# Chunk 7 of the first FFN in seven block products instead of eight, with its gate row spread later

## The chip, the cores and the metric

One core of one Trainium2 chip runs the whole program. The metric is the device time of one execution in microseconds (us). The engines are TensorE (PE in the profile, PEld its weight loads), VectorE (DVE), ScalarE (ACT), GpSimd (POOL) and SyncE (SP), whose queue issues nearly all loads of weights.

## The reference, cut to what matters

A decoder trunk of two layers over 256 tokens of width 2048, in float32. Layer 0 mixes by pooling, layer 1 by attention; each layer ends in a SwiGLU FFN of 5632 channels, and every part has a shift, a scale and a gate that are computed from a conditioning vector `c`:

```python
def swiglu(h, w_gate, w_up, w_down):
    return (jax.nn.silu(h @ w_gate) * (h @ w_up)) @ w_down
...
shift_m, scale_m, gate_m, shift_f, scale_f, gate_f = jnp.split(sc @ mod_w[i] + mod_b[i], N_MOD, axis=-1)
...
h = modulate(rmsnorm(x, norm_ffn[i]), shift_f, scale_f)
x = x + gate_f[:, None, :] * swiglu(h, ffn_gate[i], ffn_up[i], ffn_down[i])
```

The change lies in the FFN of layer 0 (`i == 0`). `gate_f` is the gate of the title; its row of 2048 numbers is the same for all tokens.

## The kernel before

**Tiles.** The 256 tokens are two token tiles of 128. The width of 2048 is four blocks `j` of 512, and the 5632 channels are 11 chunks `c` of 512. A weight block of 512x512 is one unit: 1 MB is loaded on SP's queue into one of six `raw` buffers, ACT copies its upper part (`hi`, L381) and DVE subtracts to get the lower part (`lo`, L383), each into one of six `hl` buffers. PE then makes three products (upper by upper, upper weight by lower activation, lower weight by upper activation) of four 128-deep slices for two token tiles: 24 matmuls of 128x128 by 128x512 (`proj_unit`, L406). In the last unit of a bank the first token tile's 12 matmuls come first, so that the lower part is wanted sooner.

**Order of the FFN.** A written list sets it: `p1 p0 t1 p2 t0 p3 t2 p4 p5 d0 t3 t4 p6 t5 d1 p7 t6 p8 t7 p9 t8 d2 p10 t9 d3`. `p` projects a chunk by the gate and the up weights (8 units from chunk 6 on; of chunks 0 to 5 all but the last `j` was done earlier), and DVE multiplies the silu of the one by the other (L1005). `t` turns a chunk's result so that its channels lie on the partitions: chunks 6 to 8 of layer 0 go through memory by DMAs on POOL's queue (L560, L783) and are then split (L775, L776), the others are turned by PE (L794) and split from its bank by ACT (L797) and DVE (L798). `d` multiplies a group of chunks ([0,1,2], [3,4,5], [6,7,8], [9,10]) by the down weights, and DVE adds the bank to the running sum in `x` (L807; ACT copies it in the first group, L805). Instructions are ordered by a scheduler at build time that goes by the order of the code; the splits (L381, L383) and `minus` (L879) are raised by a fixed priority. Work put on the list `pending` is written behind a later split: with the number n, n splits later.

**Background work.** The rows for later parts are computed meanwhile: `Part.unit` loads 1 MB on SP's queue into a `raw` buffer, and DVE multiplies and sums it in one instruction of 128x2048 (L222). There are 84 such units in this FFN. `tick()` at each split issues as many as a rate says, which `plan` sets as the units there are over FFN0_UNITS (87) splits.

**Seven products.** In layer 1, chunks 6 to 10 go another way (`project_in_seven`): over the two token tiles, the blocks `j` 0 and 1, and the two weights gate and up, a 2x2 by 2x2 product of blocks is made in seven block products of 12 matmuls (`seventh`, L870) instead of eight; blocks 2 and 3 stay four plain units (`whole`). So 84 + 96 = 180 matmuls stand in place of 192. It needs four differences of raw weight blocks on DVE (`minus`, 128x2048), eleven splits instead of eight, four ACT copies of single products (`kept`: L889, L899, L902, L906), and sums of token tiles. These splits don't tick. `token_sums` makes the sums of tiles once a layer, in the first down group: 14 DVE operations of 128x512 and 4 ACT copies, pended 2, 4, 6 and 8 splits on. They take an `act` buffer and the one `gate` buffer.

**The gate's row.** `gate_to` makes the row and spreads it over 128 partitions by a DMA of 1 MB on POOL's queue (L303), in layer 0 as soon as the row is there. Layer 0's sum in `x` is multiplied by it in eight DVE operations of 128x512 in `known` (L647), which are pended at the last chunk. In layer 1 (`LATE_GATES`) the load is put off until behind the seven-product chunks, and the products with the gate come behind the additions of the third down group (L979).

Of the kernel before, what the change touches and what calls it, by code (L numbers as in the profile page):

```python
# [14 lines left out]
ALU = mybir.AluOpType  # L15
AX = mybir.AxisListType

P = 128
T = 256
NT = T // P  # L20
D = 2048
# [5 lines left out]
DEPTH = 2  # L27
# [32 lines left out]
GROUPS = ([0, 1, 2], [3, 4, 5], [6, 7, 8], [9, 10])  # L60
BLOCK = 32
TURNED_BY_DMA = (range(6, 9), range(10))
SEVEN = (range(0), range(6, 11))

WIDE = 64
AM, GM = 1, 2
# [1 line left out]
GM_BY_PE = (3, 0, 1)  # L68
PAIRS = 2

LATE_GATES = ("ffn1",)

BEGUN = 6
ASIDE = 5

FFN0_UNITS, MLA_UNITS, DQ_UNITS, WO_UNITS, FFN1_UNITS = 87, 4, 6, 8, 60
DOWN_UNITS = 23

KNOWN = (1, 3, 5, 7, 9, 10, 11, 12)
# [28 lines left out]
def tile_trunk(ctx: ExitStack, tc: tile.TileContext, a: dict, out: bass.AP):  # L108
# [162 lines left out]
    pending = []  # L271
# [13 lines left out]
    def gate_to(name, first):  # L285

        col = cols[:, C_SM0, :]
        row = dram.tile([KD, P], F32, name=nm("row"))

        def spread():  # L290
            pt = ps_t()
            pe.transpose(pt[:KD, :P], col, ident)
            turned = t2k([KD, P])
            act.activation(turned, pt[:KD, :P], AF.Copy)
            act.dma_start(row, turned)
            if name in LATE_GATES:
                late_gates.append(load)
            else:
                load()

        def load():
            gates[name] = s_row if name in LATE_GATES else gate_t([P, D])
            pool.dma_start(gates[name], row.rearrange("k q -> (k q)")[None, :].to_broadcast([P, D]))  # L303

        def done(sums):
            dve.tensor_tensor(out=col, in0=sums, in1=bias(first, KD), op=ALU.add)
            pending.append((1, spread))
        return done
# [319 lines left out]
    class StreamEnd:  # L628
# [6 lines left out]
        def start(self, gate):  # L635
# [3 lines left out]
            if l == DEPTH - 1:  # L639
                self.fn = act_t([P, D], F32)  # L640
                sync.dma_start(self.fn, a["final_norm"][None, :].to_broadcast([P, D]))
        def known(self, j, tok, gate):

            js = slice(j * CH, (j + 1) * CH)
            part, piece = self.parts[tok][:, js], x[:, tok, js]
            if self.l == 0:
                dve.tensor_tensor(out=piece, in0=piece, in1=gate[:, js], op=ALU.mult)  # L647
            dve.tensor_tensor(out=part, in0=piece, in1=part, op=ALU.add)

        def piece(self, bank, tok, j):  # L650
# [107 lines left out]
    def ffn(l, hT, gate_name, begun, then):  # L758
# [169 lines left out]
        def down(i):  # L928
            g = GROUPS[i]
            last = g[-1] == NF - 1  # L930
            if i == 0 and len(SEVEN[l]):
                release(0, DOWN_UNITS)
                token_sums()
            if last:
                stat_start()
# [2 lines left out]
            for j in range(ND):  # L938
# [34 lines left out]
                for tok in range(NT):  # L973
                    if last:
                        pending.append((0, lambda bank=banks[tok], tok=tok, j=j: end.piece(bank, tok, j)))
                    else:
                        pending.append((0, lambda bank=banks[tok], sums=x[:, tok, js]: gather(bank, sums, i == 0)))
                        if gate_name in LATE_GATES and i == len(GROUPS) - 2:
                            pending.append((1, lambda sums=x[:, tok, js], gate=gates[gate_name][:, js]: dve.tensor_tensor(  # L979
                                out=sums, in0=sums, in1=gate, op=ALU.mult)))  # L980

        def project_chunk(c):
            if c == ASIDE:
                stream_aside(l)
            if c == NF - 1:
                end = StreamEnd(l)
                stream_end.append(end)
                for n, wait in enumerate(KNOWN):
                    pending.append((wait, lambda n=n: end.known(n // NT, n % NT, gates[gate_name])))
            if c in SEVEN[l]:  # L990
                nat[c] = project_in_seven(c)
                if c == GROUPS[-1][0]:
                    late_gates.pop()()
                if c in TURNED_BY_DMA[l]:
                    pending.append((0, lambda: turn_blocks(c)))
                return
# [1076 lines left out]
```

## Time and profile before

| what | value |
|---|---|
| time, median of 3 runs | 1870.15 us (1869.64 to 1870.22) |
| the profiled execution's own time | 1870.4 us |
| its span in the profile | 1868.6 us |
| granted TensorE clock, mean | 0.992 |
| TensorE busy | 1818.7 us, 97% |
| VectorE busy | 1537.7 us, 82% |
| ScalarE busy | 878.0 us, 47% |

The span is one execution between its first and its last instruction on the chip; the 1.8 us beside it lie around the program. A row of a timeline gives the start, the duration, engine, line, operation, what is written from what, shapes and count, and in brackets how long the engine had been idle and who released it. Times in a timeline are from the span's start. DVE instructions overlap a little, so what one costs a queue is the distance from its start to the next one's.

### The profile page before, as it was taken

The page shows a single profiled execution, that of the slowest core. Times are in us where ns is not written, and L with a number is a line of the kernel's source. Part 1 is how long each engine was busy: PE and PEld are TensorE (multiplying, and loading weights), DVE is VectorE, ACT ScalarE, POOL GpSimd, SP SyncE. Part 2 cuts the span into 40 slices and gives each one's busy share as a digit, 9 for nine tenths or more (in the row PEclk, how much of TensorE's full clock was granted, in tenths as well). Part 3 has the DMA queues.
Part 4 walks back from the last instruction along what each step waited for, and adds up shares of the span by engine and source line. Part 5 has one row for each costly group of instructions (what it writes and reads, how often), then busy time and mean ns, then how long its engine had stood idle before and what let it go on. Part 6 is the DMA issues. An engine that isn't in the chain of part 4 may idle for free.

```text
span 1868.6 us, 21673 instructions
## 1 busy us (share of the span) xinstructions
PE 1818.7 (97%) x8506; PEld 1480.1 (79%) x8506; DVE 1537.7 (82%) x1528; ACT 878.0 (47%) x955; POOL 67.8 (4%) x98
## 2 busy tenths in 40 slices
PE   6769999999999999999999999999999999999998
PEld 2537888888888888888889888888888888887886
DVE  1458898899889798997798885888789887898696
ACT  3225543443433343344766735643445553655353
POOL 0000000000000000000100000100011000000000
PEclk9989999999999999999999999999999999999999
DMA  9999999889999899996495394998788687458651
GB/s 391 422 422 420 415 371 339 317 310 369 409 351 421 349 400 390 393 422 231 167 382 195 132 365 172 404 380 342 299 313 321 244 325 281 180 208 319 238 225 46
DMA packets 85192, 592.27 MB, mean 317 GB/s; under 512 B 10033, under 2 KB 10465, under 8 KB 16225
## 3 DMA queue, kind: packets, MB, share of 16 engines
q1 hardware_dynamic: 79202, 570.68, 77.8%
q0 software_dynamic: 5648, 19.93, 2.9%
q8 instruction: 66, 1.08, 0.2%
q10 hardware_dynamic: 240, 0.29, 0.0%
q14 instruction: 36, 0.29, 0.0%
HBM read 576.15 MB, written 14.70 MB: 316 GB/s over the span
## 4 chain that ended last, share of the span: by engine, by line
PE 91%; DMA 4%; DVE 3%; ACT 0%; issue 0%; SPq 0%; POOL 0%; POOLq 0%; DVEq 0%; ACTq 0%
PE ps L406 73%; PE ps L870 4%; PE ps L416 2%; DMA raw<-in_mod_shift_dram 1%; PE ps L1672 1%; PE ps L249 1%; PE ps L1354 1%; DMA raw<-in_mod_scale_dram 1%; DVE hl L383 1%; DMA raw<-in_mod_wt_dram 1%; PE ps L1758 1%; PE ps L1864 1%; DVE raw L222 1%; DMA raw<-in_mod_gate_dram 1%; PE ps L1575 1%; PE ps L1214 1%
## 5 line engine op out<-in xcount | busy, mean ns | idle before, releaser
L406 PE MATMUL ps<-hl,act 128*128 128x512 f32 x6096 | 1391.3, 389 | 0.3 <-DVE act L776 0.2
L406 PEld LDWEIGHTS ps<-hl,act 128*128 128x128 f32 x6096 | 1142.6, 188 | 238.7 <-DVE act L776 0.6
L381 ACT ACTIVATE hl<-raw 128x2048 fp32r<-128x2048 f32 x297 | 566.8, 1917 | 549.0 <-PE ps L406 260.1
L383 DVE TENSOR_TENSOR hl<-raw,hl 128x2048 fp32r<-128x2048 f32 x297 | 676.2, 2285 | 119.0 <-ACT hl L381 118.5
L222 DVE SCALAR_TENSOR_TENSOR raw<-raw,s_row 128x2048 f32<-128x2048 f32 x184 | 419.1, 2282 | 3.0 <-DMA raw<-in_mod_wt_dram 2.9
L249 PE MATMUL ps<-raw,s_strip 128*32 128x512 f32 x320 | 49.0, 709 | 26.1 <-DMA raw<-in_mod_shift_dram 17.2
L870 PE MATMUL ps<-hl,act 128*128 128x512 f32 x300 | 71.6, 390 | 0.0
L741 DVE TENSOR_TENSOR act<-ps,act 128x512 f32<-128x512 f32 x80 | 53.4, 681 | 15.2 <-PE ps L406 15.1
L870 PEld LDWEIGHTS ps<-hl,act 128*128 128x128 f32 x300 | 56.2, 188 | 11.9 <-DVE hl L383 0.2
L416 PE MATMUL ps<-hl,act 128*128 128x512 f32 x192 | 47.7, 401 | 0.6 <-DVE act L512 0.5
L249 PEld LDWEIGHTS ps<-raw,s_strip 128*32 128x32 f32 x320 | 7.8, 119 | 50.6 <-issue 21.4
L879 DVE TENSOR_TENSOR raw<-raw,raw 128x2048 f32<-128x2048 f32 x20 | 45.7, 2284 | 0.3
L1214 PE MATMUL ps<-act,act 128*128 128x256 f32 x128 | 33.6, 421 | 11.5 <-issue 11.5
L1214 PEld LDWEIGHTS ps<-act,act 128*128 128x128 f32 x128 | 26.2, 211 | 21.9 <-issue 17.1
L416 PEld LDWEIGHTS ps<-hl,act 128*128 128x128 f32 x192 | 35.1, 188 | 10.3 <-ACT act L499 2.5
L560 POOL DMA_DIRECT2D turned<-t2k x32 | 17.8, 556 | 613.5 <-DVE t2k L558 613.2
L739 ACT ACTIVATE act<-ps 128x512 f32<-128x512 f32 x32 | 19.1, 597 | 38.2 <-PE ps L406 38.2
L436 ACT ACTIVATE junk<-x 128x512 bf16<-128x512 f32 x23 | 14.5, 629 | 45.7 <-DVE x L655 28.6
L529 DVE TENSOR_TENSOR hl<-raw,hl 128x2048 fp32r<-128x2048 f32 (+3 forms) x17 | 31.9, 1878 | 4.8 <-ACT hl L526 4.7
L807 DVE TENSOR_TENSOR x<-ps,x 128x512 f32<-128x512 f32 x32 | 21.5, 686 | 12.5 <-PE ps L406 12.5
L870 PE MATMUL ps<-hl,gate 128*128 128x512 f32 x120 | 29.4, 393 | 0.6 <-ACT hl L381 0.6
L1179 DVE COPY hl<-ps 128x256 f32<-128x256 f32 x4 | 1.7, 424 | 32.3 <-PE ps L1178 32.3
(277 smaller groups left out, 1217.7 us busy)
## 6 DMA issues: line engine op xcount, KB each, us to landing
raw<-in_mod_wt_dram SPq DMA_DIRECT2D x152, 1024.0 KB, 7.6
raw<-in_ffn_down_dram SPq DMA_DIRECT2D x88, 1024.0 KB, 6.8
raw<-in_ffn_gate_dram SPq DMA_DIRECT2D x86, 1024.0 KB, 6.7
raw<-in_ffn_up_dram SPq DMA_DIRECT2D x86, 1024.0 KB, 6.9
raw<-in_kv_mod_wt_dram SPq DMA_DIRECT2D x32, 1024.0 KB, 8.5
raw<-in_mod_shift_dram SPq DMA_DIRECT2D x16, 1024.0 KB, 12.4
raw<-in_w_o_dram SPq DMA_DIRECT2D x16, 1024.0 KB, 6.4
raw<-in_mod_gate_dram SPq DMA_DIRECT2D x12, 1024.0 KB, 12.5
```

Source lines behind the costliest of these rows:

```text
L222: dve.scalar_tensor_tensor(out=r, in0=r, scalar=1.0, in1=s_row, op0=ALU.mult, op1=ALU.mult, accum_out=self.sums[:, self.n:self.n + 1])
L249: pe.matmul(self.bank[m * STRIP:(m + 1) * STRIP, :], lhsT=s_strip[:, self.kt + k, :], rhs=r[:, k, i, :], start=first, stop=last)
L381: hi_ins = act.activation(hi, r, AF.Copy)
L383: lo_ins = dve.tensor_tensor(out=lo, in0=r, in1=hi.bitcast(F32), op=ALU.subtract)
L406: pe.matmul(banks[tok], lhsT=t_[:, i, k, tok * P:(tok + 1) * P], rhs=w[:, k, :], start=first and n < len(part), stop=last and n >= len(ord ...
L416: pe.matmul(bank, lhsT=t_[:, i, k, tok * P:(tok + 1) * P], rhs=w[:, k, :], start=first and n == 0, stop=last and n == len(order) - 1)
L529: dve.tensor_tensor(out=w[2][:, ks], in0=w[0][:, ks], in1=w[1][:, ks].bitcast(F32), op=ALU.subtract)
L741: dve.tensor_tensor(out=part, in0=self.banks[tok], in1=part, op=ALU.add)
L807: dve.tensor_tensor(out=sums, in0=bank, in1=sums, op=ALU.add)
L870: pe.matmul(bank, lhsT=a_(i, k), rhs=w[:, k, :], start=first and n == 0, stop=last and n == len(order) - 1, skip_group_check=read)
L879: dve.tensor_tensor(out=out, in0=a_, in1=b_, op=ALU.subtract)
L1214: pe.matmul(mixed[g][:, n % 2, :], lhsT=wp[g][:, k, ns], rhs=pool_all[g // 2][:, g % 2, k, :], start=k == 0, stop=k == KL - 1)
```

## The change

Layer 0's chunk 7 goes by `project_in_seven` too, `token_sums` runs in layer 0's first down group, and the splits that tick are 8 fewer, for which FFN0_UNITS goes from 87 to 79. The token sums take the `gate` buffer in layer 0 as well; so the spreading of the gate's row is put off until `p7`, and the eight products with the gate move from `known` into the third down group, as they stand in layer 1. In layer 0 the background list isn't empty, so `kept` are four buffers of their own.

```diff
-SEVEN = (range(0), range(6, 11))
+SEVEN = (range(7, 8), range(6, 11))
...
-LATE_GATES = ("ffn1",)
+LATE_GATES = ("ffn0", "ffn1")
...
-FFN0_UNITS, MLA_UNITS, DQ_UNITS, WO_UNITS, FFN1_UNITS = 87, 4, 6, 8, 60
+FFN0_UNITS, MLA_UNITS, DQ_UNITS, WO_UNITS, FFN1_UNITS = 79, 4, 6, 8, 60
...
-            gates[name] = s_row if name in LATE_GATES else gate_t([P, D])
+            gates[name] = s_row if name == "ffn1" else gate_t([P, D])
...
-        def known(self, j, tok, gate):
+        def known(self, j, tok):
...
-            if self.l == 0:
-                dve.tensor_tensor(out=piece, in0=piece, in1=gate[:, js], op=ALU.mult)
             dve.tensor_tensor(out=part, in0=piece, in1=part, op=ALU.add)
...
-            if i == 0 and len(SEVEN[l]):
-                release(0, DOWN_UNITS)
+            if i == 0:
+                if l == DEPTH - 1:
+                    release(0, DOWN_UNITS)
                 token_sums()
...
-                        if gate_name in LATE_GATES and i == len(GROUPS) - 2:
+                        if i == len(GROUPS) - 2:
                             pending.append((1, lambda sums=x[:, tok, js], gate=gates[gate_name][:, js]: dve.tensor_tensor(
...
-                if c == GROUPS[-1][0]:
+                if c == min(SEVEN[l][-1], GROUPS[-1][0]):
                     late_gates.pop()()
```

Below, the order of instructions is shown at three places; names carry running numbers, and from L648 on, line numbers of the changed kernel are two lower than before, and from L933 on one lower.

**DVE from the end of the first down group into chunk 6, before.** The `hl` tiles are the lower parts of the last down unit (3199) and the first four units of chunk 6 (3264, 3299, 3332, 3365), `act` tiles on L798 the turned chunks 3 and 4.

```order
L383 TENSOR_TENSOR hl_3199<-raw_3193,hl_3198 128x2048
L222 SCALAR_TENSOR_TENSOR raw_3195,sums_2981<-raw_3195,s_row 128x2048
L798 TENSOR_TENSOR act_3241<-ps_3242,act_3241 128x4x128
L798 TENSOR_TENSOR act_3241<-ps_3249,act_3241 128x4x128
L383 TENSOR_TENSOR hl_3264<-raw_3258,hl_3263 128x2048
L222 SCALAR_TENSOR_TENSOR raw_3260,sums_2981<-raw_3260,s_row 128x2048
L383 TENSOR_TENSOR hl_3299<-raw_3293,hl_3298 128x2048
L222 SCALAR_TENSOR_TENSOR raw_3295,sums_2981<-raw_3295,s_row 128x2048
L383 TENSOR_TENSOR hl_3332<-raw_3326,hl_3331 128x2048
L222 SCALAR_TENSOR_TENSOR raw_3328,sums_2981<-raw_3328,s_row 128x2048
L383 TENSOR_TENSOR hl_3365<-raw_3359,hl_3364 128x2048
```

The same stretch now, from behind the last down unit's lower part (`hl_3228`) to that of chunk 6's second unit (`hl_3328`; the third and fourth are `hl_3361` and `hl_3394`); L820 writes the lower half of a sum of tiles, L825 to L840 make the sums.

```order
L383 TENSOR_TENSOR hl_3228<-raw_3222,hl_3227 128x2048
L820 TENSOR_TENSOR act_2810<-t2k_2971,act_2810 128x512
L825 TENSOR_TENSOR t2k_3122<-act_943 128x512
L839 TENSOR_TENSOR t2k_2971<-act_1371,t2k_2971 128x512
L826 TENSOR_TENSOR t2k_3121<-t2k_3121,t2k_3122 128x512
L840 TENSOR_TENSOR t2k_2971<-t2k_2971,act_1371 128x512
L383 TENSOR_TENSOR hl_3293<-raw_3287,hl_3292 128x2048
L820 TENSOR_TENSOR gate_2811<-t2k_2971,gate_2811 128x512
L820 TENSOR_TENSOR gate_2811<-t2k_3121,gate_2811 128x512
L222 SCALAR_TENSOR_TENSOR raw_3224,sums_2928<-raw_3224,s_row 128x2048
L796 TENSOR_TENSOR act_3255<-ps_3256,act_3255 128x4x128
L383 TENSOR_TENSOR hl_3328<-raw_3322,hl_3327 128x2048
```

Seven operations of the token sums stand between these splits, and the halves of the turned chunks 3 and 4 (L796) come behind chunk 6's first units. Between `hl_3328` and `hl_3394` follow three L796, one L222, the split of `hl_3361`, and two L222 in a row.

**ACT at the start of chunk 7, before:** the upper parts of its first units, and nothing between.

```order
L381 ACTIVATE hl_3971<-raw_3966 128x2048
L381 ACTIVATE hl_4006<-raw_4001 128x2048
L381 ACTIVATE hl_4039<-raw_4034 128x2048
L381 ACTIVATE hl_4072<-raw_4067 128x2048
L381 ACTIVATE hl_4109<-raw_4104 128x2048
```

ACT there now: 4008 is the upper part of the first block, 4031 that of a whole unit, 4063 that of the block `b22` as loaded and 4080 that of `b22` after its difference; L887 copies the first product.

```order
L381 ACTIVATE hl_4008<-raw_4003 128x2048
L381 ACTIVATE hl_4031<-raw_4029 128x2048
L887 ACTIVATE t2k_3999<-ps_4007 128x512
L381 ACTIVATE hl_4063<-raw_4060 128x2048
L381 ACTIVATE hl_4080<-raw_4060 128x2048
L381 ACTIVATE hl_4098<-raw_4096 128x2048
```

The copy of the first product stands ahead of the upper part of `b22`. On DVE there now (L877 is `minus`, raw_4060 is `b22`, and L805 adds the last down banks):

```order
L383 TENSOR_TENSOR hl_4009<-raw_4003,hl_4008 128x2048
L877 TENSOR_TENSOR raw_4005<-raw_4005,raw_4003 128x2048
L805 TENSOR_TENSOR x<-ps_3896,x 128x512
L805 TENSOR_TENSOR x<-ps_3897,x 128x512
L383 TENSOR_TENSOR hl_4032<-raw_4029,hl_4031 128x2048
L383 TENSOR_TENSOR hl_4064<-raw_4060,hl_4063 128x2048
L877 TENSOR_TENSOR raw_4060<-raw_4060,raw_4005 128x2048
L877 TENSOR_TENSOR raw_4003<-raw_4060,raw_4003 128x2048
L383 TENSOR_TENSOR hl_4081<-raw_4060,hl_4080 128x2048
```

Two differences stand between the lower part of `b22` and that of its difference.

**DVE at the start of the third down group, before.** The `hl` tiles from 4907 are the lower parts of units 3 to 6 of the group; L807 adds the first pair of banks.

```order
L383 TENSOR_TENSOR hl_4907<-raw_4901,hl_4906 128x2048
L222 SCALAR_TENSOR_TENSOR raw_4903,sums_4790<-raw_4903,s_row 128x2048
L383 TENSOR_TENSOR hl_4942<-raw_4936,hl_4941 128x2048
L222 SCALAR_TENSOR_TENSOR raw_4938,sums_4790<-raw_4938,s_row 128x2048
L807 TENSOR_TENSOR x<-ps_4829,x 128x512
L807 TENSOR_TENSOR x<-ps_4830,x 128x512
L383 TENSOR_TENSOR hl_4977<-raw_4971,hl_4976 128x2048
L222 SCALAR_TENSOR_TENSOR raw_4973,sums_4790<-raw_4973,s_row 128x2048
L383 TENSOR_TENSOR hl_5010<-raw_5004,hl_5009 128x2048
```

The same four units now (4942, 4980, 5015, 5050), with the products with the gate on L978:

```order
L383 TENSOR_TENSOR hl_4942<-raw_4936,hl_4941 128x2048
L222 SCALAR_TENSOR_TENSOR raw_4938,sums_4900<-raw_4938,s_row 128x2048
L383 TENSOR_TENSOR hl_4980<-raw_4971,hl_4979 128x2048
L222 SCALAR_TENSOR_TENSOR raw_4973,sums_4900<-raw_4973,s_row 128x2048
L805 TENSOR_TENSOR x<-ps_4862,x 128x512
L222 SCALAR_TENSOR_TENSOR raw_4976,sums_4900<-raw_4976,s_row 128x2048
L805 TENSOR_TENSOR x<-ps_4863,x 128x512
L383 TENSOR_TENSOR hl_5015<-raw_5009,hl_5014 128x2048
L222 SCALAR_TENSOR_TENSOR raw_5011,sums_4900<-raw_5011,s_row 128x2048
L978 TENSOR_TENSOR x<-x,gate_4267 128x512 x2
L383 TENSOR_TENSOR hl_5050<-raw_5044,hl_5049 128x2048
```

One more background unit stands ahead of the fifth unit's lower part, and two products with the gate ahead of the sixth's. On POOL's queue the spreading of the gate's row now stands between the storing of chunk 6 and the loads that turn it, and waits for the last product that reads the token sums in the `gate` buffer.

More of the change, by code (lines that the diff above doesn't have):

```diff
@@ L988, in project_chunk @@
                 for n, wait in enumerate(KNOWN):
-                    pending.append((wait, lambda n=n: end.known(n // NT, n % NT, gates[gate_name])))
+                    pending.append((wait, lambda n=n: end.known(n // NT, n % NT)))
             if c in SEVEN[l]:
                 nat[c] = project_in_seven(c)
-                if c == GROUPS[-1][0]:
+                if c == min(SEVEN[l][-1], GROUPS[-1][0]):
                     late_gates.pop()()
```

## The prediction

> **What bounds the kernel now.** I read the page first: the sums and the chain, then the groups that the change adds to or takes from.
>
> ```profile
> span 1868.6 us, 21673 instructions
> ...
> PE 1818.7 (97%) x8506; PEld 1480.1 (79%) x8506; DVE 1537.7 (82%) x1528; ACT 878.0 (47%) x955; POOL 67.8 (4%) x98
> ...
> PE 91%; DMA 4%; DVE 3%; ACT 0%; issue 0%; SPq 0%; POOL 0%; POOLq 0%; DVEq 0%; ACTq 0%
> ```
>
> TensorE is the bound: busy in 97% of the span and 91% of the chain that ended last. A share over the whole span says nothing of one stage, so next come the stages of layer 0's FFN by windows. The columns are the stretch, its length, busy time of PE, PEld, DVE, ACT and POOL, granted clock, DMA share and GB/s; the stretches below are, in order, two in the projections ahead of the first down group, then the first down group, chunk 6, the second down group, chunk 7, the third down group and chunk 10.
>
> ```profile
> core 0: us, PE busy (x) PEld busy (x) DVE busy (x) ACT busy (x) POOL busy (x), PEclk, DMA share, GB/s
> 358.00:380.00 22.00, 22.00 (x103) 18.32 (x102) 19.45 (x16) 9.54 (x8) 0.00 (x0) 1.00 0.84 312
> ...
> 403.00:425.00 22.00, 22.00 (x102) 18.29 (x100) 20.55 (x24) 10.83 (x12) 0.00 (x0) 1.00 0.74 273
> 425.00:492.00 67.00, 67.00 (x306) 55.51 (x305) 60.33 (x48) 27.39 (x24) 0.71 (x1) 1.00 0.98 396
> 492.00:537.00 45.00, 45.00 (x205) 37.33 (x204) 35.05 (x26) 20.11 (x15) 0.00 (x0) 1.00 0.91 357
> 537.00:602.00 65.00, 65.00 (x288) 53.85 (x287) 62.04 (x50) 22.41 (x12) 2.62 (x4) 1.00 1.00 406
> 602.00:646.00 44.00, 44.00 (x195) 36.42 (x195) 32.75 (x26) 17.80 (x13) 0.00 (x0) 1.00 0.94 384
> ...
> 733.00:798.00 65.00, 65.00 (x289) 53.80 (x288) 59.43 (x46) 21.77 (x13) 0.00 (x0) 1.00 0.95 383
> 798.00:843.00 45.00, 45.00 (x204) 37.34 (x203) 44.56 (x39) 20.48 (x14) 0.00 (x0) 1.00 1.01 421
> ```
>
> TensorE has no idle time in any of them, so matmuls that go away are a gain in full, and every wait that is new is a loss in full. DVE is close behind: it idles 6.67 us in the first down group, 9.95 in chunk 6, 2.96 in the second down group, 11.25 in chunk 7 and 0.44 in chunk 10.
>
> **Twelve matmuls fewer.** The price comes from the chain of layer 1's first such chunk:
>
> ```profile
> 1478.18 2.72 PE ps L870 x12
> 1480.90 5.44 PE ps L406 x24
> ```
>
> A half product of 12 takes 2.72 us, a whole unit of 24 takes 5.44, so 0.2267 each; 192 become 180: **-2.72 us**. [...]
>
> **What DVE gets instead.** Durations by group, and costs to the queue by the distance between starts:
>
> ```profile
> L383 DVE TENSOR_TENSOR hl<-raw,hl 128x2048 fp32r<-128x2048 f32 x297 | 676.2, 2285 | 119.0 <-ACT hl L381 118.5
> L222 DVE SCALAR_TENSOR_TENSOR raw<-raw,s_row 128x2048 f32<-128x2048 f32 x184 | 419.1, 2282 | 3.0 <-DMA raw<-in_mod_wt_dram 2.9
> ...
> L879 DVE TENSOR_TENSOR raw<-raw,raw 128x2048 f32<-128x2048 f32 x20 | 45.7, 2284 | 0.3
> ```
>
> ```profile
> 735.94 2.28 DVE L222 SCALAR_TENSOR_TENSOR raw<-raw,s_row 128x2048 f32<-128x2048 f32 x1
> ...
> 738.15 2.28 DVE L383 TENSOR_TENSOR hl<-raw,hl 128x2048 fp32r<-128x2048 f32 x1
> ...
> 752.60 1.28 DVE L807 TENSOR_TENSOR x<-ps,x 128x512 f32<-128x512 f32 x2
> 753.80 2.28 DVE L383 TENSOR_TENSOR hl<-raw,hl 128x2048 fp32r<-128x2048 f32 x1
> ...
> 758.21 2.28 DVE L383 TENSOR_TENSOR hl<-raw,hl 128x2048 fp32r<-128x2048 f32 x1
> ```
>
> A big operation costs 2.21 us (735.94 to 738.15), a 128x512 one 0.60 (two from 752.60 to 753.80). Chunk 7 gets three more splits, four differences and five small additions: 7 x 2.2 + 5 x 0.6 = 18.4 us. The token sums are 14 x 0.60 = 8.4 us in the first down group and chunk 6. Chunk 7 loses its eight ticks, 8 x 84/87 = 7.7 background units or 17.1 us; these go to the other splits, 84/79 - 84/87 = 0.098 unit or 0.22 us more for each 5.44 us of TensorE. Totals fit into DVE's idle time. But DVE works in order, so what counts is whether the next lower part still comes before TensorE wants it. The wants come from TensorE's rows; 24 products are 5.44 us, and the runs count the units:
>
> ```profile
> 452.54 27.50 PE L406 MATMUL ps<-hl,act 128*128 128x512 f32 x120
> ...
> 480.67 5.71 PE L406 MATMUL ps<-hl,act 128*128 128x512 f32 x24
> ...
> 487.01 32.93 PE L406 MATMUL ps<-hl,act 128*128 128x512 f32 x144
> ...
> 520.57 305.02 PE L406 MATMUL ps<-hl,act 128*128 128x512 f32 x1344
> ...
> 1478.01 2.88 PE L870 MATMUL ps<-hl,act 128*128 128x512 f32 x12
> ...
> 1488.92 2.88 PE L870 MATMUL ps<-hl,act 128*128 128x512 f32 x12
> ```
>
> *First down group.* The 120 are its units 6 to 10, the 144 its last and chunk 6's first five. Unit 6 begins at 452.54 and wants its lower part eight products on, at 454.4.
>
> ```profile
> 449.40 2.29 DVE L383 TENSOR_TENSOR hl<-raw,hl 128x2048 fp32r<-128x2048 f32 x1
> ...
> 455.52 2.29 DVE L383 TENSOR_TENSOR hl<-raw,hl 128x2048 fp32r<-128x2048 f32 x1 [1.62 <-ACT hl L381]
> ```
>
> It is there at 451.7, 2.7 us early. The new order puts two more background units and one small sum ahead of it since the FFN began, 2 x 2.21 + 0.60 = 5.0 us. DVE's idle time in the stretches 358 to 380 and 403 to 425 (2.55 + 1.45) can take 4.0 of that. I take 0, with 0 to 2.3 (5.0 - 2.7) for the range.
>
> *Chunk 6's fourth unit* begins four units behind 487.01, at 508.8, and in the new order wants its lower part 12 products on, at 511.5.
>
> ```profile
> 486.85 1.09 ACT L797 ACTIVATE act<-ps 128x512 fp32r<-128x512 f32 x2 [3.45 <-PE ps L794]
> ```
>
> The upper half of the second token sum stands on ACT behind these copies of chunk 4's turned bank: done at about 487.9 + 0.6 = 488.5. From there DVE's new order can be walked: five small ones, to 491.5; the first unit's lower part, to 493.7; two small, one background, one small, to 497.7; the second's, 499.9; three small, one background, the third's, 506.1; two background units and the fourth's, 512.7. So TensorE waits **1.25 us**. Before, it ended early:
>
> ```profile
> 504.04 2.28 DVE L383 TENSOR_TENSOR hl<-raw,hl 128x2048 fp32r<-128x2048 f32 x1
> ```
>
> 506.3, 5.2 ahead of that want. Ahead of it now stand two background units and 14 small operations more than before, 12.8 us, of which 5.0 were counted above and 7.8 come after 455. Bounds: 0, and 7.8 - 5.2 = 2.6 if none of DVE's later idle time gives way. At the start of the second down group three lower parts are just in time by the same walk: **0.1**.
>
> *Chunk 7.* In layer 1, ACT's rows at the same place, TensorE beginning the chunk at 1478.01:
>
> ```profile
> 1477.31 1.92 ACT L381 ACTIVATE hl<-raw 128x2048 fp32r<-128x2048 f32 x1 [1.21 <-PE ps L406]
> ...
> 1480.93 0.60 ACT L889 ACTIVATE t2k<-ps 128x512 f32<-128x512 f32 x1 [1.23 <-PE ps L870]
> ...
> 1483.97 3.72 ACT L381 ACTIVATE hl<-raw 128x2048 fp32r<-128x2048 f32 x2 [2.44 <-DVE raw L879]
> ```
>
> There the upper part of `b22` (1477.31) precedes the copy of the first product; in layer 0 it stands behind it. The chain from the chunk's start T: first product done T + 2.7, copy to T + 3.5, upper part to T + 5.4, its lower part to T + 7.6, difference to T + 9.8, the upper part of that to T + 11.7; TensorE wants it behind 12 + 24 + 12 products, at T + 10.9, and waits 0.8 to 0.9. The lower part, behind a second difference, comes at T + 14.3; it is wanted ten products after T + 11.8, at T + 14.1. Together **1.1 us**. Bounds: 0, since in layer 1 the same stretch has no wait (the third product starts at 1488.92, 10.9 behind the start) and one of its chunks is full,
>
> ```profile
> 1584.00:1625.00 41.00, 41.00 (x183) 33.79 (x182) 34.35 (x16) 23.19 (x17) 0.00 (x0) 1.00 0.52 195
> ...
> 1666.00:1709.00 43.00, 42.23 (x185) 34.16 (x184) 40.08 (x27) 25.16 (x20) 2.62 (x4) 1.00 0.60 221
> ```
>
> while another lost 0.77; and 1.6 without the two products of the next unit that the scheduler put between.
>
> *Third down group.* 1344 products from 520.57 are three units of chunk 6, twelve, 24 and twelve units, and five; so this group begins 39 units on, at 733.0, its sixth unit at 760.2 and wants its lower part at 762.8. That ended at 760.5 (758.21 + 2.28), 2.3 early. New ahead of it: one background unit, two products with the gate and a small one of 128x16, 2.2 + 1.2 + 0.1 = 3.5. So **1.2 us**; bounds 0 to 1.4.
>
> **At nothing.** The 8 x 0.60 = 4.8 us of products with the gate leave chunk 10 and the last group, where TensorE doesn't wait now: a relief of an engine that is ahead. The spread of the gate's row leaves the first down group for chunk 7:
>
> ```profile
> gate<-row POOLq DMA_DIRECT2D x2, 1024.0 KB, 8.6
> ```
>
> It waits there for the last half product on the token sums, some T + 25, lands by T + 35, and on POOL's queue holds back the two loads that turn chunk 6. Behind those, ACT's queue holds the silu and the third upper part of chunk 8; the latter is wanted at T + 52, which covers some 10 us. The eight ACT copies stand in the chains above or in ACT's idle half.
>
> **Sum:** -2.72 + 1.25 + 0.1 + 1.1 + 1.2 = +0.9. On the profiled execution's 1870.4 that is 1871.3; the median of the runs is 0.25 lower, so **1871.1 us**. A measurement of this kernel can tell about 0.2% from no change, 3.7 us: under 1866.4 is faster, over 1873.9 slower. The forecast is no change; its own range, with the waits' 3.65 us between half and one and a half of that, is 1869.3 to 1872.9.
>
> **Rivals.**
>
> *No wait is new.* The lower parts stay ahead everywhere, as in layer 1's chunk from 1584: 1870.15 - 2.72 = 1867.4. For it speaks DVE's idle time in the stretches from 425 and 492 (16.6 us, against 12.8 us more work up to the fourth unit of chunk 6). Against it speaks that this idle time is a wait for ACT, which stays. 0.22.
>
> *DVE's idle time can't be used, slower.* One mechanism: each pause of DVE is a wait for an upper part, ACT's upper parts wait for TensorE to free an `hl` buffer, and so work added ahead only delays. Places: the first down group, 5.0 - 2.7 = 2.3, and chunk 6's fourth unit, 2.6; then 0.1, 1.1 and 1.2 as above. 7.3 - 2.72 = +4.6: 1874.7. It decides (over 1873.9) where of the idle time ahead of these two places less than 0.9 us gives way. The waits for ACT speak for it:
>
> ```profile
> DVE hl L383 <- ACT hl L381: 30.4, 19, 5.8
> ```
>
> 30.4 us over 358 to 880. Against it: at 455.52 the upper part was late by ACT's own queue and not by TensorE. 0.20.
>
> *The loads become the bound.* Weights and background are 1 + 84/79 = 2.06 units of 1.049 MB per 5.44 us in the down groups, 398 GB/s. If that couldn't be carried, one unit more in each of the first two groups, 2.6 us each at 406 GB/s, would come on top: 1871.1 + 5.2 = 1876.3. Chunk 10's row carries 421 GB/s and the second group's 406. [...] 0.04.
>
> *More gain than the matmuls*, as the last stages start with DVE's relief: under 1866.4, though no row shows TensorE waiting there. 0.04.
>
> **How the numbers follow.** Forecast 0.50, the rivals 0.22, 0.20, 0.04, 0.04. No change: 0.50 + 0.22 = 0.72; slower 0.20 + 0.04 = 0.24; faster 0.04. The range reaches from the first rival to the second, each with 0.2 of scatter: 1867.2 to 1874.9; the other two, 0.08, stay out.
>
> **What would show it.** Right: idle time of PE ended by DVE's L383 near 511 (about 1.2 us), by ACT's L381 and DVE's L383 11 to 14 us into chunk 7 (1.1), and at the third down group's sixth unit (1.2); chunk 7 with 180 products; a full PE elsewhere. Wrong: no PE idle at these places (then 1867.4), or idle time already near 455. The forecast is wrong altogether if PE's time per product changes, or if the waits lie in ACT's queue behind the silu of chunk 7.

## The result, and the profile after

The changed kernel takes 1878.99 us (median of 5, 1878.75 to 1879.59), the kernel before beside it 1869.64: 9.35 us more, ratio 1.0052 [1.0041, 1.0063]. The forecast was 1871.1 with a range to 1874.9. It is slower, outside the range and past the furthest rival (1876.3).

The page of the profile after:

```profile
span 1877.3 us, 21669 instructions
...
PE 1818.5 (97%) x8494; PEld 1477.1 (79%) x8494; DVE 1563.4 (83%) x1554; ACT 886.6 (47%) x966; POOL 67.8 (4%) x98
...
PE 85%; DVE 8%; DMA 4%; issue 2%; ACT 1%; SPq 0%; DVEq 0%; POOL 0%; POOLq 0%; ACTq 0%
```

TensorE has 12 matmuls less and yet the same busy time. A sum over the whole program hides the stages: TensorE was busy 2.0 us longer in this FFN in the changed trace, but 2.2 us longer ahead of it in the trace before, where the clock was lower at the program's start (0.83 between 100 and 150 us, against 0.86). DVE's share of the chain rose from 3% to 8%. The windows of the same stages:

```profile
425.00:492.00 67.00, 64.07 (x284) 52.48 (x283) 58.46 (x50) 28.20 (x26) 0.00 (x0) 0.97 0.92 368
492.00:537.00 45.00, 42.73 (x190) 34.47 (x189) 44.97 (x39) 19.88 (x17) 0.00 (x0) 1.00 0.87 335
537.00:602.00 65.00, 64.87 (x286) 53.02 (x285) 62.49 (x50) 24.24 (x13) 1.26 (x2) 1.00 1.01 421
602.00:646.00 44.00, 43.04 (x189) 34.96 (x188) 38.75 (x22) 23.55 (x16) 2.06 (x3) 1.00 0.69 269
...
733.00:798.00 65.00, 63.30 (x278) 51.65 (x277) 59.66 (x51) 22.16 (x13) 0.00 (x0) 1.00 0.93 373
798.00:843.00 45.00, 45.00 (x204) 37.33 (x204) 42.98 (x40) 17.41 (x12) 0.00 (x0) 1.00 1.01 420
```

Where TensorE was busy throughout, it now idles 2.93, 2.27, 0.13, 0.96 and 1.70 us, and in the first down group its mean clock is 0.97. TensorE's timeline names these waits:

```profile
448.62 0.28 PE L292 MATMUL ps<-con,cols 128*16 128x128 f32 x1 [2.69 <-DVE cols L306]
...
490.68 20.57 PE L406 MATMUL ps<-hl,act 128*128 128x512 f32 x88 [0.24 <-ACT hl L381]
511.70 4.83 PE L406 MATMUL ps<-hl,act 128*128 128x512 f32 x20 [0.46 <-DVE hl L383]
518.33 8.48 PE L406 MATMUL ps<-hl,act 128*128 128x512 f32 x36 [1.80 <-DVE hl L383]
...
621.87 2.12 PE L868 MATMUL ps<-hl,act 128*128 128x512 f32 x8 [0.96 <-ACT hl L381]
...
646.77 122.03 PE L406 MATMUL ps<-hl,act 128*128 128x512 f32 x536
770.50 63.77 PE L406 MATMUL ps<-hl,act 128*128 128x512 f32 x280 [1.70 <-DVE hl L383]
```

Three of the places are those of the forecast: chunk 6's fourth unit, chunk 7's difference, the third down group's sixth unit. The first is not: TensorE stands at L292, the small transposition that turns the finished gate column, until DVE has made the column (L306). Before, the column was made at 449.29 and TensorE came to it at 452.52:

```profile
449.29 0.17 DVE L306 TENSOR_TENSOR cols<-sums,vcol 128x16 f32<-128x16 f32 x1
```

```profile
452.52 0.27 PE L292 MATMUL ps<-con,cols 128*16 128x128 f32 x1
```

Now it is made at 448.38, when TensorE has stood there since 445.9:

```profile
448.38 0.18 DVE L306 TENSOR_TENSOR cols<-sums,vcol 128x16 f32<-128x16 f32 x1
```

Some idle time has no name there (the 0.13 us of the second down group), and a lower clock is no wait. Nor is the named idle time all that a wait takes: the 20 products from 511.70 are worth 4.5 us, and the next one starts 6.63 us on, 2.1 us late, of which 1.80 is named. So I took from each trace the start of the first product of each stage, and the difference to before, stage by stage, in one execution each (us; "first group a" is its first six units; a number is what the stage lost):

| kernel | first group a | b | chunk 6 | second group | chunk 7 | chunks 8, 9 | third group | chunk 10 | last group | sum |
|---|---|---|---|---|---|---|---|---|---|---|
| changed | 4.48 | 0.50 | 3.23 | 0.67 | -1.15 | -0.10 | 2.35 | -0.03 | 0.04 | 9.95 |
| row_later | 2.19 | 0.71 | 3.13 | 0.68 | -1.14 | -0.10 | 2.39 | -0.01 | 0.01 | 7.86 |
| rate_only | 2.24 | -0.03 | 0.03 | 0.69 | 0.00 | 1.47 | 0.01 | 0.82 | 0.18 | 5.41 |
| sums_later | 2.24 | -0.02 | 0.04 | 0.84 | -1.15 | -0.10 | 2.37 | -0.04 | 0.04 | 4.18 |
| copy_behind | 4.28 | 0.54 | 3.13 | 0.68 | -2.66 | -0.10 | 2.35 | 0.00 | 0.00 | 8.18 |
| gate_known | 2.85 | 0.54 | 3.15 | 0.69 | -1.14 | -0.10 | 1.16 | 0.00 | 0.00 | 7.12 |
| late_rate | 0.01 | 0.53 | 4.77 | 0.00 | -1.15 | -0.10 | 4.16 | 2.75 | 0.03 | 10.96 |
| all4 | 1.59 | 0.13 | 0.03 | 0.84 | -2.66 | -0.10 | 1.14 | -0.04 | 0.04 | 0.94 |
| late_all | -0.15 | 0.13 | 0.03 | 0.00 | -2.66 | -0.10 | 3.25 | 2.27 | 0.03 | 2.77 |
| paced | -0.15 | 0.07 | 0.78 | 0.00 | -2.58 | 6.88 | -0.01 | 0.00 | 2.15 | 7.14 |
| paced_flat | -0.15 | 0.10 | 0.78 | 0.00 | -2.45 | 1.45 | -0.01 | 3.59 | 0.06 | 3.37 |
| paced_even | -0.15 | 0.10 | 0.78 | 0.00 | -0.99 | 0.71 | 0.08 | 0.13 | 0.04 | 0.70 |

So the changed kernel loses 9.95 in this FFN. Its span is only 8.7 longer, since the trace before, with its lower clock at the start, came to this FFN 1.3 us later; behind the FFN both take 987.0. The lower rows are the experiments, told next. The medians below move with these sums, give or take 2 us (paced 3.3): a table row is one execution, and those of one kernel differ, as will be seen.

**The clock.** Behind the wait at L292 the windows (444 to 454) of the changed kernel, and then of `gate_known`, which has the same instructions up to there and waits the same 2.69 us:

```profile
444.00:447.00 3.00, 1.93 (x9) 1.27 (x7) 3.00 (x4) 0.77 (x1) 0.00 (x0) 1.00 0.94 396
447.00:449.00 2.00, 0.38 (x3) 0.34 (x4) 2.00 (x4) 0.72 (x1) 0.00 (x0) 1.00 1.00 422
449.00:452.00 3.00, 3.00 (x10) 2.36 (x9) 3.00 (x2) 1.20 (x1) 0.00 (x0) 0.60 1.04 429
452.00:454.00 2.00, 2.00 (x8) 1.56 (x7) 2.00 (x3) 0.73 (x1) 0.00 (x0) 0.74 1.00 422
```

```profile
449.00:452.00 3.00, 3.00 (x15) 2.45 (x14) 3.00 (x2) 0.77 (x1) 0.00 (x0) 1.00 1.00 423
452.00:454.00 2.00, 2.00 (x11) 1.65 (x10) 2.00 (x3) 1.16 (x1) 0.00 (x0) 1.00 1.01 426
```

The granted clock falls to 0.60 and 0.74 in the one and stays at 1.00 in the other: 18 products in 5 us against 26. That is the 1.6 us between 4.48 and 2.85 in the table. From the rows, 0.40 x 3 + 0.26 x 2 = 1.7 us of clock are lost; from 450 to 452 the row has 0.50. `copy_behind` waits the same 2.69 us and pays too (0.50 from 449 to 451, and 4.28 in the table). So the same wait of 2.69 us costs clock in two executions and none in a third; what makes the difference is not shown.

### The profile page after: what moved, and what is told of

Its sections match the earlier page's. It is cut to its first block, busy times and chain, and to the rows that moved or that the text cites. A ratio compares the mean times of both kernels' runs of the same rounds, so it can differ in the third digit from the quotient of the medians.

```text
span 1877.3 us, 21669 instructions
## 1 busy us (share of the span) xinstructions
PE 1818.5 (97%) x8494; PEld 1477.1 (79%) x8494; DVE 1563.4 (83%) x1554; ACT 886.6 (47%) x966; POOL 67.8 (4%) x98
## 4 chain that ended last, share of the span: by engine, by line
PE 85%; DVE 8%; DMA 4%; issue 2%; ACT 1%; SPq 0%; DVEq 0%; POOL 0%; POOLq 0%; ACTq 0%
PE ps L406 66%; PE ps L868 5%; DVE hl L383 3%; DVE raw L222 2%; PE ps L416 2%; DMA raw<-in_mod_shift_dram 1%; PE ps L1671 1%; PE ps L249 1%; PE ps L1353 1%; DMA raw<-in_mod_scale_dram 1%; DMA raw<-in_mod_wt_dram 1%; PE ps L1757 1%; PE ps L1863 1%; DMA raw<-in_mod_gate_dram 1%; PE ps L1574 1%
## 5 line engine op out<-in xcount | busy, mean ns | idle before, releaser
L383 DVE TENSOR_TENSOR hl<-raw,hl 128x2048 fp32r<-128x2048 f32 x300 | 683.6, 2289 | 102.3 <-ACT hl L381 101.9
L222 DVE SCALAR_TENSOR_TENSOR raw<-raw,s_row 128x2048 f32<-128x2048 f32 x184 | 420.0, 2289 | 2.3 <-DMA raw<-in_mod_wt_dram 2.3
L249 PE MATMUL ps<-raw,s_strip 128*32 128x512 f32 x320 | 48.6, 703 | 27.2 <-DMA raw<-in_mod_shift_dram 17.0
L877 DVE TENSOR_TENSOR raw<-raw,raw 128x2048 f32<-128x2048 f32 x24 | 54.9, 2287 | 0.4
L436 ACT ACTIVATE junk<-x 128x512 bf16<-128x512 f32 x23 | 14.5, 630 | 46.0 <-DVE x L653 28.9
L868 PE MATMUL ps<-hl,gate 128*128 128x512 f32 x144 | 35.2, 392 | 0.6 <-ACT hl L381 0.6
L868 PEld LDWEIGHTS ps<-hl,gate 128*128 128x128 f32 x144 | 27.0, 188 | 6.8 <-ACT hl L381 1.0
L805 DVE TENSOR_TENSOR x<-ps,x 128x512 f32<-128x512 f32 x32 | 21.5, 690 | 11.0 <-PE ps L406 11.0
```

What stands on the lines that cost most here:

```text
L222: dve.scalar_tensor_tensor(out=r, in0=r, scalar=1.0, in1=s_row, op0=ALU.mult, op1=ALU.mult, accum_out=self.sums[:, self.n:self.n + 1])
L249: pe.matmul(self.bank[m * STRIP:(m + 1) * STRIP, :], lhsT=s_strip[:, self.kt + k, :], rhs=r[:, k, i, :], start=first, stop=last)
L383: lo_ins = dve.tensor_tensor(out=lo, in0=r, in1=hi.bitcast(F32), op=ALU.subtract)
L805: dve.tensor_tensor(out=sums, in0=bank, in1=sums, op=ALU.add)
L868: pe.matmul(bank, lhsT=a_(i, k), rhs=w[:, k, :], start=first and n == 0, stop=last and n == len(order) - 1, skip_group_check=read)
L877: dve.tensor_tensor(out=out, in0=a_, in1=b_, op=ALU.subtract)
```

## The experiments

Each ran five rounds beside the kernel before; times are medians. Two theories went in: A, each wait has its own cause in DVE's or ACT's order; B, DVE is short as a whole, so a wait that is taken away comes back further on.

**row_later**

```diff
-            pending.append((1, spread))
+            pending.append((5 if name == "ffn0" else 1, spread))
```

> Edit: in layer 0 TensorE's transposition of the gate column (L292) is pended five splits behind the column instead of one; the rest as changed (1879.0). Theory A, each place on its own: the first down group loses 4.5 us because TensorE stands in order at this transposition until DVE has worked through two background units (2.7 us idle, then 1.8 us at a lower granted clock), so the time is 1874.5 and the other waits (near 490 to 518, in chunk 7, near 770) keep their size. Theory B, one shortage: DVE is behind as a whole, TensorE meets it 4.5 us sooner and waits that much longer at the first token sums and in chunk 6, so the time stays at 1877.5 to 1879.5.

1877.76 against 1869.19, ratio 1.0043 [1.0031, 1.0056]. The median lies in B's range, but the stages are neither's. In its trace L292 doesn't wait, and TensorE meets the lower parts instead:

```profile
450.48 3.92 PE L406 MATMUL ps<-hl,act 128*128 128x512 f32 x16 [1.26 <-DVE hl L383]
454.89 9.36 PE L406 MATMUL ps<-hl,act 128*128 128x512 f32 x40 [0.49 <-DVE hl L383]
```

The stage keeps 2.19 of its 4.48: DVE itself is 2.2 us late there, and the transposition only turned that into one long wait, behind which the clock fell to 0.50. Chunk 6 keeps 3.13 and doesn't grow, as B would have it; it and the rest keep their size, as A has it.

**rate_only**

```diff
-FFN0_UNITS, MLA_UNITS, DQ_UNITS, WO_UNITS, FFN1_UNITS = 87, 4, 6, 8, 60
+FFN0_UNITS, MLA_UNITS, DQ_UNITS, WO_UNITS, FFN1_UNITS = 79, 4, 6, 8, 60
```

in the kernel before, and nothing else.

> Edit: the kernel before, with FFN0_UNITS at 79 instead of 87 and nothing else: all eight-product chunks, no token sums, but the background 10% denser and done eight splits sooner. Theory A: the 4.5 us of the first down group come from the denser background alone (its part ends a unit sooner on TensorE's queue and DVE is two units of work later): 1869.6 + 3 to 4.5 = 1872.6 to 1874.1, with TensorE's wait before L292 in the trace and chunk 6 without a wait. Rival: the token sums make DVE late; then this is 1869.6 plus or minus 0.7.

1875.15 against 1869.19, ratio 1.0028 [1.0018, 1.0039]: 6 us from the density alone, more than A expected. The trace has the wait at L292 without any token sum (and chunk 6 without a wait), and two more behind, in chunk 9 and ahead of the last group, where the changed kernel loses nothing:

```profile
448.27 0.28 PE L292 MATMUL ps<-con,cols 128*16 128x128 f32 x1 [2.08 <-DVE cols L306]
...
714.21 131.06 PE L406 MATMUL ps<-hl,act 128*128 128x512 f32 x576 [0.84 <-ACT hl L381]
...
846.85 2.11 PE L406 MATMUL ps<-hl,act 128*128 128x512 f32 x8 [0.70 <-ACT act L797]
```

So 2.24 of the first group's loss is the denser background's. It ends the gate's sums one unit sooner in TensorE's order, but no sooner on DVE: L292 stands behind the group's fourth unit instead of its fifth, 21.8 us behind the group's start instead of 27.2, and the column is done 24.0 behind it (24.1 before). In the changed kernel it is done at 24.6, for the first small operation of the token sums, 0.60, stands ahead of it; that makes 2.85, and the clock 4.48. The second group's 0.69 is the density's too; of rate_only's 5.4 in the table, only these two are losses of the changed kernel.

**sums_later**: layer 0's token sums pended 12, 14, 16 and 18 splits on.

```diff
-            for wait, f in ((2, lambda: join(0, (0, 1), (1, 1), ALU.add)), (4, second), (6, fourth),
+            waits = (2, 4, 6, 8) if l else (12, 14, 16, 18)
+            for wait, f in ((waits[0], lambda: join(0, (0, 1), (1, 1), ALU.add)), (waits[1], second), (waits[2], fourth),
...
```

> Edit: in layer 0 the four token sums are pended 12, 14, 16 and 18 splits behind the start of the first down group instead of 2, 4, 6 and 8, so that they stand one by one between the splits of chunk 6; the rest as changed (1879.0). Theory A: chunk 6 loses 3.7 us because nine operations of the sums and the turned chunks' copies stand together ahead of its first four lower parts; spread out, under 1 us of it is left, while the second down group, whose start had 0.7, loses up to 1: 1876 to 1877. Theory B: the same work in DVE's queue costs the same further on, 1878.5 to 1880.

1875.26 against 1869.19, ratio 1.0033 [1.0021, 1.0045]. Chunk 6 loses 0.04 instead of 3.23; the second group 0.84 instead of 0.67. A holds, and the time is below its range, since the first group loses less as well (2.24: no sum ahead of the column, and the clock stayed at 1.00). Why the sums cost so much where they stood can be read in the changed kernel's DVE timeline:

```profile
483.69 0.69 DVE L825 TENSOR_TENSOR t2k<-act,act 128x512 f32<-128x512 f32 x1 [6.43 <-PE ps L792]
484.30 2.28 DVE L383 TENSOR_TENSOR hl<-raw,hl 128x2048 fp32r<-128x2048 f32 x1
...
489.31 0.69 DVE L820 TENSOR_TENSOR act<-t2k,act 128x512 fp32r<-128x512 f32 x1
...
493.92 0.69 DVE L820 TENSOR_TENSOR act<-t2k,act 128x512 fp32r<-128x512 f32 x1
...
515.97 2.30 DVE L383 TENSOR_TENSOR hl<-raw,hl 128x2048 fp32r<-128x2048 f32 x1
```

The second operation of the first sum needs a buffer of the `t2k` ring, and those hold chunks 3 to 5 until TensorE has turned chunk 3 (L792). DVE, in order, stands 6.43 us at it, with splits and background behind; the first sum's lower half is at 489.31, the second's at 493.92. Pended behind the turning, the sums find buffers. The run doesn't separate this wait from the mere number of operations that stood there together.

**copy_behind**

```diff
-            later(lambda: act.activation(kept[0], u1, AF.Copy))
+            pending.append((0 if l else 1, lambda: act.activation(kept[0], u1, AF.Copy)))
```

> Edit: in layer 0 the copy of chunk 7's first product is pended one split more, so that on ACT it stands behind the upper part of b22; the rest as changed (1879.0). Theory A: the wait of chunk 7 (0.96 us for ACT and some 0.6 beside it) is this order alone; it goes, 1877.4. Theory B: DVE, not ACT, is late there by its two differences, and the time stays at 1878.5 to 1879.3.

1876.98 against 1869.19, ratio 1.0041 [1.0029, 1.0054]: A. Chunk 7 gives -2.66 instead of -1.15: the whole price of the seven products, 12 x 0.2267, arrives. In the changed kernel ACT stood idle at that copy, and the upper part of `b22` came behind it, at 613.25, 3.4 us into the chunk (which begins at 609.84):

```profile
612.76 0.60 ACT L887 ACTIVATE t2k<-ps 128x512 f32<-128x512 f32 x1 [5.06 <-PE ps L868]
613.25 1.91 ACT L381 ACTIVATE hl<-raw 128x2048 fp32r<-128x2048 f32 x1
619.91 5.52 ACT L381 ACTIVATE hl<-raw 128x2048 fp32r<-128x2048 f32 x3 [4.75 <-DVE raw L877]
```

In copy_behind `b22` was there already and its upper part ran 0.7 us ahead of the chunk (609.11):

```profile
608.41 1.92 ACT L381 ACTIVATE hl<-raw 128x2048 fp32r<-128x2048 f32 x1 [1.57 <-PE ps L406]
```

**gate_known**: layer 0's products with the gate back in `known`, none of them in the third down group.

```diff
-                        if i == len(GROUPS) - 2:
+                        if l and i == len(GROUPS) - 2:
...
+            if self.l == 0:
+                dve.tensor_tensor(out=piece, in0=piece, in1=gate[:, js], op=ALU.mult)
```

> Edit: layer 0's eight products with the gate go back from the third down group to the additions behind chunk 10, where they stood before; the rest as changed (1879.0, 9.4 over before). Theory A, each place on its own: the third down group's 2.35 us come from the two products and the one background unit ahead of its sixth lower part; without the products 1.2 of it go and what is left is at most 0.6, so 1876.8 to 1877.3, and chunk 10 and the last group don't wait. Theory B: the denser background alone makes that wait, and 1.5 us or more of it stay: 1878 or more.

1876.72 against 1869.18, ratio 1.0042 [1.0029, 1.0055]. The third group loses 1.16 instead of 2.35, the two products' 1.2 us to the tenth; chunk 10 doesn't mind them. What stays is twice A's 0.6 and less than B's 1.5. It goes with the place of the background unit between the two additions: rate_only, as dense but without a second unit there, loses 0.01.

**late_rate**: the changed kernel with FFN0_UNITS at 87, and behind `project_in_seven` in layer 0

```diff
+                if l == 0:
+                    release(goal[0], 35)
```

> Edit: as changed, but the background keeps its old pace (84 units over 87 splits) until chunk 7, and what is left is spread over the 35 splits behind it (1.19 a split). Theory A: the denser background ahead of chunk 7 is the larger cause. The wait in the first down group (4.5) goes, chunk 6 keeps 1 to 2.6 of its 3.2 for the token sums, the second down group is back to 0.2, chunk 7 stays at -1.15, and the third down group grows from 2.35 to 3 or 3.5: 1869.2 + 4 to 5.5 = 1873 to 1875. Rival: DVE's total is the limit, and what leaves the front comes back behind chunk 7, 1877.5 or more.

1879.85 against 1869.18, ratio 1.0058 [1.0046, 1.0071]. The front is as expected (0.01 in the first group, 0.00 in the second), but what left it comes back: 4.16 in the third group and 2.75 in chunk 10, and chunk 6, which loses 4.77 with the token sums at the old density, had a lower clock behind its wait (0.50 from 516 to 518). The rival was right on the sum.

**all4**: row_later, sums_later, copy_behind and gate_known in one.

> Edit: the transposition of the gate column five splits later, the token sums at 12 to 18 splits, the first product's copy one split later and the products with the gate behind chunk 10, all in one; the background as dense as changed. Theory A: the stages add up: 2.2 in the first down group (as with the sums moved or the transposition moved), 0 in chunk 6, 0.8 in the second down group, -2.7 in chunk 7, 0.1 to 0.6 in the third: +0.4 to +0.9, 1869.6 to 1870.2, and up to 1.8 more in executions where TensorE's clock falls behind a wait. Theory B: 1873 or more, as the lower parts stay late in another place.

1870.19 against 1869.18, ratio 1.0006 [0.9997, 1.0015]. The sum is A's (0.94), with less in the first group and more in the third than A had, and 8 of the 9.4 us are gone with the same arithmetic on the same engines; the time isn't told from before. What is left, 1.59, 0.84 and 1.14, stands at places that the runs above put down to the denser background, but for some 0.15 that the later sums add in the second group.

**late_all**: those four and late_rate.

> Edit: the four edits together and the background at its old pace until chunk 7, the rest of it spread over the 35 splits behind. Theory A: no wait ahead of chunk 7 (0 to 0.3), -2.7 in chunk 7, 0 to 1.5 in the third down group for 1.19 units a split: 1866.5 to 1868.3, the first kernel below before. Rival: DVE has no room for the 7.7 units in the stages behind chunk 7, and loses 3 us or more there: 1870 or more.

1872.49 against 1869.18, ratio 1.0018 [1.0009, 1.0026]: the rival's time. 1.19 units a split lose 3.25 and 2.27 in the third group and chunk 10. That DVE is what has no room is not shown: of the four waits of TensorE that are named in these stages, two end with lower parts (0.91 and 0.81) and two with ACT's upper parts (1.16 and 0.75), and in the trace before chunk 10's window had a DMA share of 1.01 and 421 GB/s already, without a wait.

**The paces.** Three kernels with the four edits and a written list of background units for each split; two ticks were added ahead of chunk 7's last unit. All have 84 units.

```diff
     def tick():
+        if pace:
+            pump(pace.pop(0))
+            return
...
+        if l == 0:
+            pace.extend([...])
```

| units in | chunks 0 to 5 (12 splits) | first group (12) | chunk 6 (8) | second group (12) | chunk 7 (2) | chunk 8 (8) | chunk 9 (8) | third group (12) | chunk 10 (8) |
|---|---|---|---|---|---|---|---|---|---|
| paced | 11 | 11 | 7 | 12 | 2 | 12 | 8 | 12 | 9 |
| paced_flat | 12 | 11 | 7 | 13 | 3 | 9 | 8 | 12 | 9 |
| paced_even | 12 | 11 | 8 | 13 | 2 | 9 | 8 | 13 | 8 |

> Edit: the four edits together, and layer 0's background written out split by split instead of one rate: 0.92 a split ahead of chunk 6, none at the first split of the second and third down groups, two in chunk 7's last whole units, 1.5 a split in chunk 8, where lower parts were up to 10 us early, 1 in chunks 9 and 10 and the third group; 84 units as before. Theory A (a lower part is late only where background stands ahead of it just behind a chunk's end or in the first down group): the stages lose 0 to 0.3 each, chunk 7 gives -2.7, and the time is 1866.5 to 1868, under before's 1869.2. Theory B (behind chunk 7 DVE has no room for more than 1.06 units a split, as with 1.19): chunk 8's extra units come back as 2 us or more in chunk 9 or the third group, 1869.5 or more.

1879.50 against 1869.09, ratio 1.0056 [1.0042, 1.0069]: worse than either theory. The front, but for chunk 6, and the third group lose nothing any more; the last group waits 1.75 for DVE's half of a turned chunk, behind chunk 10's two last units. Chunks 8 and 9 lose 6.9, at ACT's upper parts, for which TensorE waits four times from 664.99 to 686.76 (0.26, 1.03, 1.78 and 1.75), and the loads that these wait for (30.3 us of ACT's idle time over 640 to 700); the window has a DMA share of 1.01:

```profile
667.00:689.00 22.00, 17.45 (x75) 13.48 (x74) 21.32 (x19) 5.73 (x3) 0.00 (x0) 1.00 1.01 417
```

> Edit: as the paced kernel, but chunk 8's twelve units become nine (1.1 a split, what the loads carry: 2.1 units of 1.049 MB in 5.44 us are 405 GB/s, where 2.5 would have been 482 over the 422 seen), chunk 7 three instead of two, the second down group 13, chunk 10's last split none, so that nothing stands ahead of the last turned chunk. Theory A (loads bound chunk 8 there, and DVE's order chunk 10): the stages lose 0 to 0.4 each, chunk 7 gives -2.7 to -2: 1866.8 to 1868.5, under before's 1869.1. Theory B (the 7.7 units have no room anywhere without a wait): the 5 us come back in chunks 8 to 10, 1870.5 or more.

1871.56 against 1869.26, ratio 1.0012 [1.0003, 1.0021]: B's range. Chunk 8 is down to 1.35; chunk 10, with nine units in eight splits and two of them first, loses 3.59, with waits for ACT's upper parts (0.66, 0.79 and 1.24) and the DMA share at 1.01 again:

```profile
798.00:843.00 45.00, 42.31 (x188) 34.15 (x187) 42.67 (x38) 18.21 (x13) 0.00 (x0) 1.00 1.01 421
```

> Edit: as the paced kernels, with one background unit a split nearly everywhere: none at the first split of the second and third down groups (13 units in each of these twelve-split groups, the doubled ones late), 11 in the first, two in chunk 7, nine in chunk 8, eight in chunks 6, 9 and 10. Theory A (up to 1 a split behind a chunk's end costs nothing, 1.2 a split costs what the loads can't carry): stages lose 0 to 0.4, chunk 7 gives -2.6: 1867 to 1868.3 against 1869.2. Theory B (there is no pace without a wait at the density that seven products need): 1869.5 or more.

1868.27 against 1869.03, ratio 0.9995 [0.9986, 1.0004]: in A's range by a hair, but not told from before, though the median is the only one below it. Its profiled execution was the slowest of its eleven, 1870.28, and lost 1.6 in chunk 7 to an upper part that the other kernels with that order had in time; the others lay between 1867.57 and 1868.98.

## Why the prediction was wrong, by its steps

The forecast's sum was +0.9. In its own terms the trace has -2.72 + 4.98 (first group, a and b) + 3.23 + 0.67 + 1.57 (chunk 7) + 2.35, or about +10. Half of the miss is the first down group; of its 4.98 the last 0.50, with a wait for an upper part (490.68), is in no term of the forecast.

- **Twelve matmuls, -2.72.** Right: -2.66 where nothing covers it (copy_behind, all4).
- **First down group, "I take 0, with 0 to 2.3".** This step failed most: 4.48. The idle time that was to take 4.0 us was hardly used: in the stretches 358 to 380 and 403 to 425 DVE idled 2.55 and 1.45 us before, and 2.23 and 1.55 in the changed kernel. So DVE was late by 2.2 (row_later): for the lower part the bound was right and the value at the wrong end. Missed altogether was that TensorE itself waits for the end of a background part, at L292, and that the denser rate moves that a unit forward in its order (2.85, gate_known); and that behind this wait of 2.69 us the clock fell to 0.50, which cost 1.6 us more.
- **The denser background counted as 0.22 us a unit that DVE's idle time takes.** Alone it costs 6 us (rate_only), 2.24 and 0.69 of it in the first and second groups as in the changed kernel, the rest further on. It had two ends with one value. The rival "DVE's idle time can't be used" (0.20, 1874.7) comes nearest, but it was priced without L292 and the clock, and it holds for the first group only: in the window of chunk 6 DVE's idle time fell from 9.95 to 0.03. No run tests its reason, that ACT's upper parts wait for TensorE.
- **Chunk 6, 1.25.** 3.23, and the place was right. The token sums make it: 0.03 at the new density without them (rate_only), 4.77, part of it clock, with them at the old one (late_rate). The walk's steps were right, but not where it began, at 488.5, when ACT was done with the second sum's upper half. In the changed trace this stage begins 3.7 us later (-1.3 + 4.48 + 0.50), so that is 492.2 there; the second sum's lower half came at 493.92, nearly 1.8 later. The fourth unit's lower part, told for 512.7, which is 516.4 there, was done at 518.3, as late as the start. 1.25 + 1.8, and what a wait takes beside its named time, are about the 3.23. DVE came late by the first sum's 6.43 us at a buffer, as its timeline has it. The order shows what stands ahead, not which buffer it needs.
- **Second down group, 0.1.** 0.67. The denser background makes it: 0.69 with that alone (rate_only), 0.00 at the old density (late_rate).
- **Chunk 7, 1.1.** 1.5 to 1.6, in the way that was told (0.96 is named, 621.87): ACT's upper part of the difference was done 12.0 behind the start (told: 11.7), the lower part 14.5 (14.3).
- **Third down group, 1.2.** 2.35. The two products with the gate cost what was counted (1.19, gate_known). Mis-sized was the time at which the sixth unit's lower part is wanted, told for 762.8, 2.6 us into the unit. TensorE stopped for it after eight products: of the 536 from 646.77, 24 are chunk 7's last unit, 384 chunks 8 and 9, and 120 the group's first five units. Eight are 1.8 us, so the lower part had been 1.5 us early and not 2.3, and 3.5 of new work leave 2.0; the rest is what a wait takes beside its named time.
- **At nothing.** Held: no wait at the gate's row or behind it, chunk 10 and the last group lost and gained nothing.
- **The loads**, with 0.04, did not bind at 1.06 units a split: in the changed kernel's second down group the DMA engines moved 421 GB/s, and TensorE idled 0.13 us. At 1.1 to 1.5 the waits of TensorE lead to ACT's upper parts, and from there to loads in paced (417 GB/s); in paced_flat the window beside them has 421 GB/s, and what these upper parts waited for is not shown.

Not settled: why the three paces still lose 0.8 in chunk 6 (in paced_even's trace at its last unit, where TensorE stands until the lower part is there, at 533.23, with 0.30 named), and why the upper part in its profiled chunk 7 came late.

## What to carry to other kernels

Work that leaves one stage of a balanced kernel goes somewhere: price the place that receives it first, here eight units of background into stages where the second engine was 90 to 95% busy (the down groups), and not by the mean of its idle time. Look for everything of the bounding engine that waits for the receiving one, small transpositions at the end of background work too, and for each moved operation, which buffer ring it draws from and who frees that. And four edits of order alone, none of which touched the arithmetic, were worth 8 of the 9.4 us.

## What the runs showed of the hardware

TensorE's granted clock fell behind a single wait of 2.69 us in two of the three traces with that wait, to 0.50 from 450 to 452 in the changed kernel and from 449 to 451 in copy_behind, and stayed at 1.00 in gate_known; in late_rate it fell behind waits of 0.43 and 1.79 within 8 us:

```profile
511.00:514.00 3.00, 1.21 (x7) 0.67 (x5) 3.00 (x4) 1.10 (x1) 0.00 (x0) 1.00 0.91 339
514.00:516.00 2.00, 2.00 (x7) 1.58 (x8) 2.00 (x1) 0.60 (x1) 0.00 (x0) 0.72 1.02 406
516.00:518.00 2.00, 2.00 (x6) 1.61 (x5) 2.00 (x3) 0.00 (x0) 0.00 (x0) 0.50 1.00 422
```

In the changed kernel the same 1.80 at 518 cost no clock, with 1.00 from 518 to 524, nor did 2.59 in row_later's chunk 6 (1.00 from 501 to 507). So one execution doesn't show the whole price of the wait at L292: 1.6 us of clock came on top in the changed kernel, 1.4 in copy_behind and none in gate_known. The executions of sums_later spread by 3.1 us and those of paced by 4.6, where the kernel before spreads by 1 to 2; that the clock makes this spread is not shown, for the mean clocks of these executions don't follow their times (sums_later's fastest has 0.989, its slowest 0.994).
